# A hybrid decoder layer on one core: the gate's first weights, the routing's order and the final sums rearranged

## The chip, the cores and the metric

The kernel runs on one core of a Trainium2 chip, with its engines TensorE (PE), VectorE (DVE), ScalarE (ACT), GpSimd (POOL) and SyncE (SP), which here issues most loads. The metric is the device time of one execution in microseconds. Three executions of the kernel before took 1488.31, 1494.20 and 1494.39 us, median 1494.2.

## The reference

One decoder layer on 512 tokens of width 2048, in float32. A state-space group and a convolution group share one input projection; their outputs, side by side, go through one output projection. Then come a layer normalisation, a mixture of 32 experts, a second normalisation, a gated embedding and a third normalisation:

```python
h = layer_norm(DEEPNORM_ALPHA * x + y, ln1_g[i], ln1_b[i])
m = hierarchical_moe(h, w_rg[i], b_rg[i], w_re[i], b_re[i], w_gate[i], w_up[i], w_down[i])
h = layer_norm(DEEPNORM_ALPHA * h + m, ln2_g[i], ln2_b[i])
e = (p[i] @ w_p[i]) * jax.nn.sigmoid(h @ w_pg[i] + b_pg[i])
x = layer_norm(DEEPNORM_ALPHA * h + e, ln3_g[i], ln3_b[i])
```

In the mixture each token picks one of four groups by a softmax over 4 logits, two of that group's eight experts by a softmax over their logits, and adds the two experts' outputs with those weights. An expert is `silu(t @ w_gate) * (t @ w_up)` (width 256), times the weight, times `w_down`.

## The kernel before

Tokens lie in four tiles of 128 (`tt`, 2048 columns each). The program runs on five engines, each in its own order, with semaphores between them; the order on each engine is set by a scheduler that works through the code below with a timeline of its own, and by the pools of buffers, whose reuse makes waits.

Up to about 630 us: input projection, the two groups, output projection. Then the first normalisation of the four tiles, written to `h_dram`, and the routing on VectorE: the experts' one-hots (`oh`), counts and ranks by matmuls (`cc`, `cn`, `rk`), ranks of the experts by load (`gt`), each token's place (`hot`), and by matmul the slots' token rows (`sl0`) and weights (`wt0`). The embedding `p @ w_p` is computed in pieces (`embedding`, later L1177) and stored to `p_dram`. Its weights lie in the two raw places (`wps`).

The expert stage works in 14 groups of up to four experts with 128 slots in all. For a group GpSimd gathers 128 token rows from `h_dram` into `gx` (L1070), TensorE transposes them (L1084), multiplies with four quarters of `w_gu` (L1104, `up`), VectorE and ScalarE form the activations (`act`), TensorE multiplies with the two halves of `w_dn` (L1124, `down`), and GpSimd scatters each half of the result to `y_dram` (L1074), where every token has two rows. Each expert takes six loads of 1 MB, 192 in all. SyncE issues them in order (`ring_load`, L1066) into a ring of 17 places (15 of the stage's own and the two raw places, which join when the embedding's weights are done). Behind group 0, program text L1161 to L1181, stand the embedding of tiles 2 and 3 and the scaling of `tt` by ALPHA. Then comes a branch (L1189) for a case of overflow, which this data doesn't take; at it each engine waits for its own outstanding transfers.

The final stage loads each tile's two rows per token from `y_dram`, adds them to `tt`, takes statistics (L1334), normalises (L158 to L181), transposes (L1348), splits into a high and a low half (`h2h`, `h2l`, L79 and L80) and multiplies with the gate's weights `w_pg` (16 loads of 1 MB, split the same way into `whi` and `wlo`), three matmuls for each product (L100 to L102). The first four of these loads go to the two raw places and two places `fr`, with half of the splits on GpSimd. GpSimd also adds most of the rows (L1332, L1333).

Of the kernel before, what the change touches and what calls it, by code (L numbers as in the profile page):

```python
# [54 lines left out]
def build(tc, I, out, dbg=None, stages=9):  # L55
# [159 lines left out]
    sl0 = cpool.tile([P, 2 * NGR], I32, name="sl0")  # L215
    wt0 = cpool.tile([P, NGR], FT, name="wt0")
# [421 lines left out]
    if True:  # L638

        yhl = []  # L640

        def y_rows(n):

            y2 = s1.enter_context(tc.tile_pool(reuse_waits="tile", name=f"y2{n}", bufs=1))
            yhl.append([[y2.tile([P, 8, 2 * P], FR, name=f"y{n}{a}{g}") for a in "hl"] for g in range(2)])
# [139 lines left out]
        with ExitStack() as s3:  # L785
            w_o = ahead([lambda c=c, q=q: wsplit(wB if q % 2 else wA, raw_load(I["w_o"][c, q]), 4) for c in range(4) for q in range(2, 4)], 3)
            op_ = s3.enter_context(tc.tile_pool(reuse_waits="tile", name="op", bufs=1, side="right"))
            st1 = [op_.tile([P, 4, 6], FT, name=f"st{m}") for m in range(NT)]
# [39 lines left out]
            def embedding(m, x):  # L828

                z = op_.tile([P, 1], FT, name="pz0", bufs=1)  # L830
                V.tensor_scalar(z, x, 0.0, 0.0, op0=OP.is_equal, op1=OP.mult)
                pm = wB.tile([P, 2, P], FT, name="pm", tag="whi", bufs=4)
                A.activation(pm, pT[:, :, m * P:(m + 1) * P], AF.Identity, bias=z)
                for q in range(2):
                    pe_ = wB.tile([P, 2, 512], FT, name="pe", tag="wlo", bufs=4)
                    for c in range(2):
                        ps = bank("ops")
                        for k in range(2):
                            T.matmul(ps, pm[:, k], wps[q][:, k, c * 512:(c + 1) * 512], start=k == 0, stop=k == 1)
                        A.copy(pe_[:, c], ps)  # L840
                    G.dma_start(p_dram[m, 2 * q:2 * q + 2].rearrange("c p d -> p c d"), pe_)
# [19 lines left out]
            def finish(m):  # L861
                mean, rstd = ln_stats(op_, st1[m], "s")
                nm = op_.tile([P, 1], FT, name="nm", bufs=1)
                V.scalar_tensor_tensor(nm, mean, -1.0, rstd, op0=OP.mult, op1=OP.mult)
                lt = op_.tile([P, 36], FT, name="lt", bufs=2)
                V.scalar_tensor_tensor(lt, s12[:, 0:36], nm, s12[:, 36:72], op0=OP.mult, op1=OP.add)
                V.scalar_tensor_tensor(lg[:, m], lacc[m], rstd, lt, op0=OP.mult, op1=OP.add)
                if m < NT - 2:
                    normalize(m, mean, rstd)
                return m, mean, rstd  # L870

            def normalize(m, mean, rstd):
                for q in range(4):
                    i = slice(q * 512, (q + 1) * 512)
                    t = tt[m][:, i]
                    layer_norm(t, t, mean, rstd, g1[:, i], b1[:, i])
                G.dma_start(h_dram[m * P:(m + 1) * P], tt[m])
                dump("h", tt[m], lambda d: d[m * P:(m + 1) * P])
# [29 lines left out]
            pT = wB.tile([P, 2, S], FT, name="pT", tag="whi", bufs=4)  # L908
# [12 lines left out]
            rank = place[:, 0]  # L921
            gl = lg[:, :, 0:4]
            el = lg[:, :, 4:36]
            gmax, gsum, gprob, gmin = rt("gmax", NT), rt("gsum", NT), rt("gprob", NT), rt("gmin", NT)
            V.tensor_reduce(gmax, gl, axis=AX.X, op=OP.max)
            gmb = gmax.unsqueeze(2).broadcast_to([P, NT, 4])
            gd, ge, gs_, pen = rt("gd", NT, 4), rt("ge", NT, 4), rt("gs", NT, 4), rt("pen", NT, 4)
            V.tensor_tensor(gd, gl, gmb, op=OP.subtract)
            exp_of(rp, ge, gd, [P, NT, 4], "eg")
            V.tensor_reduce(gsum, ge, axis=AX.X, op=OP.add)  # L930
            V.reciprocal(gprob, gsum)

# [44 lines left out]
            V.tensor_scalar(gt, krow, kcol, None, op0=OP.is_lt)  # L977
            rr, rc = bank("ops"), bank("ops")
# [14 lines left out]
            embedding(0, rtok[:, 0:1])  # L993
# [44 lines left out]
            A.dma_start(sv_dram, sv.rearrange("p a n -> p (a n)"))  # L1038
            embedding(1, wt0[:, 0:1])
# [8 lines left out]
    if True:  # L1048
        psE = s5.enter_context(tc.tile_pool(reuse_waits="tile", name="psE", bufs=1, space=PSUM))
# [5 lines left out]
        def big(name):  # L1055
            return ep.tile([P, D], FT, name=name)

        ring = [big(f"ring{n}") for n in range(2, NRING)]
        xt = ep.tile([P, KD, P], FT, name="xt")
        gx, ob = big("gx"), big("ob")  # L1060
        turn = [0]
# [44 lines left out]
        def act(gu, w):  # L1106
            act = ep.tile([P, FH], FT, name="act")
            at = ep.tile([P, 2, P], FT, name="at", bufs=2)
# [40 lines left out]
        pm = ep.tile([P, 2, 2 * P], FT, name="pm")  # L1149
        nc.sync.dma_start(pm, I["pT"][:, :, 2 * P:])  # L1150
        gather(sl0[:, 0:1])
        V.tensor_copy(ids_, tab[:, 0:NP])
        columns()
        for i, (width, members) in enumerate(GROUPS):
# [11 lines left out]
            if i:  # L1166
                continue

            ahead1 = [loads(1, 0)]

            for m in range(2):
                for q in range(2):
                    pe_ = ep.tile([P, 2, 512], FT, name="pe")
                    for c in range(2):
                        ps = bank("dps", 4)
                        for k in range(2):
                            T.matmul(ps, pm[:, k, m * P:(m + 1) * P], wps[q][:, k, c * 512:(c + 1) * 512], start=k == 0, stop=k == 1)  # L1177
                        (A.copy if c else V.tensor_copy)(pe_[:, c], ps)
                    G.dma_start(p_dram[2 + m, 2 * q:2 * q + 2].rearrange("c p d -> p c d"), pe_)
            for m in range(NT):  # L1180
                A.mul(tt[m], tt[m], ALPHA)  # L1181
            ring.extend(rpool.tile([P, D], FT, name="raw", tag="raw", bufs=2) for _ in range(2))
            ahead1.append(loads(1, 1))

# [59 lines left out]

    s5.close()


    with ExitStack() as s5:
# [22 lines left out]

        raws = [rpool.tile([P, D], FT, name="raw", tag="raw", bufs=2) for _ in range(2)] + [fy.tile([P, D], FT, name=f"fr{n}") for n in range(2)]
        for q in range(3):
            nc.sync.dma_start(raws[q], I["w_pg"][0, q])
        y0 = [fy.tile([P, 2, 1024], FT, name=f"y0{c}") for c in range(2)]
        hls = [wsplit(wF, raws[q], 8, (V, V) if q else (G, G)) for q in range(3)]
# [41 lines left out]
        def total(m):  # L1318

            t = h2[m]  # L1320
            st2 = fh.tile([P, 4, 6], FT, name="st2", bufs=2)
            if m:
                rs = [rpool.tile([P, 2, 1024], FT, name="raw", tag="raw", bufs=2) for _ in range(2)]
                for c in range(2):
                    load_y(rs[c], m, c)
            else:
                rs = y0
            for c, r in enumerate(rs):
                for q in range(2):
                    i = slice(q * 512, (q + 1) * 512)  # L1330
                    o = t[:, c * 1024 + q * 512:c * 1024 + (q + 1) * 512]
# [23 lines left out]
        fystk.close()  # L1355
        fp = s5.enter_context(tc.tile_pool(reuse_waits="tile", name="fp", bufs=1))
# [109 lines left out]
```

## Time and profile before

| | |
|---|---|
| median of three executions | 1494.2 us |
| the profiled execution's own time | 1491.18 us |
| its span in the profile | 1489.4 us |
| busy: PE, DVE, POOL, ACT | 1264.2, 784.9, 394.9, 373.5 us |
| mean granted clock of TensorE | 0.932 of full speed |
| read from memory, written | 324.49 MB, 36.38 MB |

The profile is of one execution; durations below are of that one. A row with x4 merges four instructions, and its time runs from the first one's start to the last one's end. The bracket at a row's end is the idle time of the engine ahead of it and what ended that. SPq and the like are an engine's own queue work, such as issuing a DMA.

### The profile page before, as it was taken

The numbers are of one execution on the slowest core, as the hardware profiler recorded it, in microseconds if no ns is written. First come the engines' busy times: TensorE is split into PE (matmuls) and PEld (weight loads), VectorE is DVE, ScalarE is ACT, GpSimd is POOL, SyncE is SP. The second block draws the span as 40 slices with busy tenths as digits, with TensorE's granted clock in tenths as the row PEclk, the third lists the DMA queues.
The fourth block names the chain that finished last, engine by engine and source line by source line (L and its number), as shares of the span: only waits on it lengthen the run. The fifth ranks groups of instructions, "written<-read, shape, count | busy, mean of one in ns | idle before, by whom it ended". The sixth has DMA issues, their size and how long they took to land.

```text
span 1489.4 us, 16537 instructions
## 1 busy us (share of the span) xinstructions
PE 1264.2 (85%) x6128; PEld 809.5 (54%) x6129; DVE 784.9 (53%) x1258; ACT 373.5 (25%) x562; POOL 394.9 (27%) x330
## 2 busy tenths in 40 slices
PE   6999999999999999966758989987767675599996
PEld 4877877777777888843213333332111122388884
DVE  7999899789997643680101111110000006975567
ACT  4336555554333421121001111110000003023210
POOL 0368677864944200001101111100000005600000
PEclk9999999998999999958969999999998996699998
DMA  6344444436531351536779999999999985426413
GB/s 233 110 131 119 152 145 136 144 113 217 219 122 57 114 209 57 227 141 260 300 273 420 417 400 421 421 421 418 419 411 415 417 359 203 141 99 219 140 44 120
DMA packets 97176, 349.47 MB, mean 235 GB/s; under 512 B 30136, under 2 KB 43960, under 8 KB 61504
## 3 DMA queue, kind: packets, MB, share of 16 engines
q1 hardware_dynamic: 51152, 303.34, 52.6%
q10 hardware_dynamic: 38160, 19.82, 5.1%
q0 software_dynamic: 7776, 25.18, 4.3%
q8 instruction: 50, 0.82, 0.2%
q14 instruction: 38, 0.31, 0.1%
HBM read 324.49 MB, written 36.38 MB: 242 GB/s over the span
## 4 chain that ended last, share of the span: by engine, by line
PE 24%; DMA 19%; DVE 5%; issue 1%; ACT 1%; POOL 0%; DVEq 0%; SPq 0%; POOLq 0%
DMA ring<-w_gu 12%; PE gu L1104 7%; DMA ring<-w_dn 6%; PE dps L1124 4%; PE fps L102 3%; PE fps L100 3%; PE fps L101 3%; PE xtp L1084 1%; DMA gx<-h_dram,sl 1%; DVE tt L180 1%; DVE tt L181 1%; PE h2p L102 0%; PE h2p L100 0%; PE h2p L101 0%; DVE lnq L166 0%
## 5 line engine op out<-in xcount | busy, mean ns | idle before, releaser
L1104 PE MATMUL gu<-ring,xt 128*32 128x512 f32 (+2 forms) x1032 | 231.3, 634 | 42.6 <-DMA ring<-w_gu 42.6
L236 DVE SCALAR_TENSOR_TENSOR cps<-hc,wdw,cps 128x512 f32<-128x512 f32 x232 | 174.4, 752 | 4.8
L100 PE MATMUL zp<-xh,whi 128*128 128x512 f32 x384 | 157.7, 412 | 10.2 <-ACT whi L79 10.2
L79 ACT CAST whi<-raw 128x1024 fp32r<-128x1024 f32 x116 | 119.4, 1047 | 170.3 <-PE zp L102 51.3
L1104 PEld LDWEIGHTS gu<-ring,xt 128*32 128x32 f32 (+2 forms) x1032 | 62.6, 129 | 176.7 <-issue 101.5
L80 DVE TENSOR_TENSOR wlo<-raw,whi 128x1024 fp32r<-128x1024 f32 x90 | 126.6, 1416 | 57.4 <-ACT whi L79 56.4
L102 PE MATMUL zp<-xh,wlo 128*128 128x512 f32 x384 | 154.2, 402 | 3.0 <-DVE wlo L80 3.0
L101 PE MATMUL zp<-xl,whi 128*128 128x512 f32 x384 | 154.7, 403 | 1.6 <-DVE xl L80 1.6
L1124 PE MATMUL dps<-ring,at 128*32 128x512 f32 (+2 forms) x584 | 132.3, 619 | 13.0 <-DMA ring<-w_dn 6.5
L1110 DVE TENSOR_TENSOR act<-act,gu 128x256 f32<-128x256 f32 x14 | 5.9, 422 | 217.0 <-ACT act L1109 217.0
L1074 POOL DMA_INDIRECT y_dram<-ob,sl x28 | 27.9, 995 | 321.7 <-ACT ob L1126 321.7
L1089 DVE COPY xt<-xtp 128x512 f32<-128x512 f32 x28 | 19.4, 692 | 155.6 <-PE xtp L1084 146.9
L80 POOL TENSOR_TENSOR wlo<-raw,whi 128x1024 fp32r<-128x1024 f32 x26 | 69.5, 2675 | 87.2 <-ACT whi L79 74.7
L100 PE MATMUL fps<-whi,h2h 128*128 128x512 f32 x224 | 89.8, 402 | 1.0 <-ACT h2h L79 1.0
L102 PE MATMUL fps<-whi,h2l 128*128 128x512 f32 x224 | 89.8, 402 | 0.0
L101 PE MATMUL fps<-wlo,h2h 128*128 128x512 f32 x224 | 89.1, 399 | 0.0
L1124 PEld LDWEIGHTS dps<-ring,at 128*32 128x32 f32 (+2 forms) x584 | 38.2, 128 | 91.6 <-issue 63.2
L100 PEld LDWEIGHTS zp<-xh,whi 128*128 128x128 f32 x384 | 73.5, 192 | 25.9 <-ACT whi L79 10.3
L102 PEld LDWEIGHTS zp<-xh,wlo 128*128 128x128 f32 x384 | 73.3, 191 | 21.1 <-DVE wlo L80 4.2
L101 PEld LDWEIGHTS zp<-xl,whi 128*128 128x128 f32 x384 | 73.6, 192 | 17.2 <-DVE xl L80 2.0
L1126 DVE COPY ob<-dps 128x512 f32<-128x512 f32 x28 | 19.4, 692 | 111.9 <-PE dps L1124 106.4
L1084 PE MATMUL xtp<-ident,gx 128*128 128x128 f32 x224 | 38.2, 296 | 44.3 <-DMA gx<-h_dram,sl 32.5
(451 smaller groups left out, 2283.6 us busy)
## 6 DMA issues: line engine op xcount, KB each, us to landing
ring<-w_gu SPq DMA_DIRECT2D x109, 1024.0 KB, 20.7
ring<-w_dn SPq DMA_DIRECT2D x61, 1024.0 KB, 19.8
raw<-w_in SPq DMA_DIRECT2D x24, 1024.0 KB, 5.0
raw<-w_gu SPq DMA_DIRECT2D x19, 1024.0 KB, 20.1
raw<-w_o SPq DMA_DIRECT2D x16, 1024.0 KB, 5.0
raw<-w_pg SPq DMA_DIRECT2D x14, 1024.0 KB, 5.1
raw<-y_dram SPq DMA_DIRECT2D x12, 512.0 KB, 5.6
raw<-xT SPq DMA_DIRECT2D x4, 1024.0 KB, 5.1
```

The costliest lines, as they stand in the source:

```text
L79: A.copy(hi, src)
L80: eng.tensor_tensor(lo, src, hi.bitcast(FT), op=OP.subtract)
L100: T.matmul(ps, lh, rh, start=start, stop=False)
L101: T.matmul(ps, lh, rl, start=False, stop=False)
L102: T.matmul(ps, ll, rh, start=False, stop=stop)
L236: V.scalar_tensor_tensor(ps if k < 30 else acc, hc[:, k:k + S], wdw[:, ct, k:k + 1], ps, op0=OP.mult, op1=OP.add)
L1074: G.indirect_dma_start(out=y_dram[q], out_offset=bass.IndirectOffsetOnAxis(ap=isc, axis=0), in_=ob[:, q * 1024:(q + 1) * 1024], in_offset= ...
L1084: T.transpose(ps[:, kk * P:(kk + 1) * P], gx[:, k * P:(k + 1) * P], ident)
L1089: V.tensor_copy(o, ps)
L1104: T.matmul(gu[cols], xt[:, k, cols], raws[j][:, kk * 512:(kk + 1) * 512], start=k == 0, stop=k == KD - 1)
L1124: T.matmul(outs[c][cols], at[:, k, cols], raws[j][:, o:o + 512], start=k == 0, stop=k == 1)
L1126: (A.copy if c else V.tensor_copy)(ob[:, q * 1024 + c * 512:q * 1024 + (c + 1) * 512], outs[c])
```

## The change

1. Of the first normalisation, tiles 2 and 3 are taken out of the stretch ahead of the routing and given to VectorE in pieces between the routing's steps, each held back by a value of the step it follows. The exponentials of the weights follow the slots' rows. The first gather takes its rows from a copy of its own, `sl1`, and the clearing of `gx` goes.
2. The embedding is cut into pieces of half a tile. Six of eight stand ahead of the experts, the last three of them stored from ScalarE's queue; tile 3's two stand behind group 1's `down`, on the raw places' weights. Scaling by ALPHA moves to group 2.
3. The ring has another order: 15 places in `ep` and two `kept` places in a pool that lives on into the final stage. The raw places join at its head behind tile 3's embedding. The last 17 loads pass over the kept and raw places, which take the gate's first four loads.
4. In the final stage, tile 0's first rows and all rows of the other tiles are added into `tt` by GpSimd's accumulating DMAs, tile 0's second rows by a plain load and VectorE. Tiles 1 to 3 wait at a one-column instruction for tile 0. The splits on GpSimd go to ScalarE and VectorE.

The diff, cut to its core:

```diff
+            embedding(0, 0, lacc[NT - 1][:, 0:1])
...
-            for d in done[NT - 2:]:
-                normalize(*d)
+            for q in range(2):
+                normalize(2, q, *done[2], oh[:, 0, 0:1])
...
+            for q in range(4):
+                normalize(3, q, *done[3], hot[:, 0, 0:1])
...
+            V.tensor_scalar(sl1, sz[:, 0:1], float(S - 1), None, op0=OP.min)
+            for n, (m, q) in enumerate(((1, 1), (2, 0), (2, 1))):
+                embedding(m, q, sz[:, n:n + 1], A)
...
+        kept = [kp.tile([P, D], FT, name=f"kept{n}") for n in range(2)]
+        ring = [ring[0], *ring[4:], *kept, last, ring[1], ring[2], ring[3]]
...
         def ring_load(src):
-            t = ring[turn[0] % NRING]
-            turn[0] += 1
+            count[0] += 1
+            t = ring.pop(0)
+
+            while count[0] > 6 * NE - NRING and any(t is k for k in kept):
+                t = ring.pop(0)
+            ring.append(t)
             nc.sync.dma_start(t, src)
...
-            for m in range(2):
+            if i == 1:
+
                 for q in range(2):
...
+                kept += [rpool.tile([P, D], FT, name="raw", tag="raw", bufs=2) for _ in range(2)]
+                ring[:0] = kept[2:]
...
+        for q in range(4):
+            V.tensor_copy(kept[q][:, 0:1], at_[(NGR + 1) % 2][:, 0, 0:1])
+            nc.sync.dma_start(kept[q], I["w_pg"][0, q])
...
+        def add_y(m, j):
+
+            for c in range(2):
+                G.dma_start(h2[m][:, c * 1024:(c + 1) * 1024], yv[c][m, :, j], accum_op=OP.add)
...
+        add_y(0, 0)
+        for m in range(1, NT):
+
+            o = h2[m].rearrange("p (c d) -> p c d", c=2)[:, :, 0]
+            V.scalar_tensor_tensor(o, h2[0][:, 0:2], 0.0, o, op0=OP.mult, op1=OP.add)
+        for m, j in ((1, 0), (2, 0), (1, 1), (3, 0), (2, 1), (3, 1)):
+            add_y(m, j)
+        hls += [wsplit(wF, kept[q], 8) for q in range(2, 4)]
...
-                    (G if m or q == 0 else V).tensor_tensor(r[:, 0, i], r[:, 0, i], r[:, 1, i], op=OP.add)
-                    (G if m and not (m == 1 and q) else V).tensor_tensor(o, o, r[:, 0, i], op=OP.add)
-                    V.bn_stats(st2[:, 2 * c + q], o)
+            for q in range(4):
+                o = t[:, q * 512:(q + 1) * 512]
+                if m == 0:
+                    V.tensor_tensor(o, o, y1[:, q * 512:(q + 1) * 512], op=OP.add)
+                V.bn_stats(st2[:, q], o)
```

Three places of the instruction order, each before and after. On SyncE at the branch (L1189), before; a load's target is a place of the ring or a raw place, with a buffer's number behind it, and register instructions between the loads are left out.

```order
L1066 DMA ring8_5521<-w_dn 128x2048
L1066 DMA raw_5695<-w_gu 128x2048
L1066 DMA raw_5696<-w_gu 128x2048
L1189 UNCONDITIONAL_BRANCH
L1066 DMA ring9_5522<-w_gu 128x2048
L1066 DMA ring10_5523<-w_gu 128x2048
L1066 DMA ring11_5524<-w_gu 128x2048
L1066 DMA ring12_5525<-w_gu 128x2048
L1066 DMA ring13_5526<-w_dn 128x2048
```

And now (the branch is L1233):

```order
L1112 DMA ring10_5573<-w_dn 128x2048
L1112 DMA ring11_5574<-w_dn 128x2048
L1233 UNCONDITIONAL_BRANCH
L1112 DMA raw_6359<-w_gu 128x2048
L1112 DMA raw_6360<-w_gu 128x2048
L1112 DMA kept0_5585<-w_gu 128x2048
L1112 DMA kept1_5586<-w_gu 128x2048
L1112 DMA ring12_5583<-w_dn 128x2048
L1112 DMA ring1_5564<-w_dn 128x2048
L1112 DMA ring2_5565<-w_gu 128x2048
```

The raw loads have moved from ahead of the branch to behind it, where they precede all other loads. Each waits for the last matmul of tile 3's embedding (L1216) that reads its place.

On SyncE at the end of the expert stage, before: the last expert loads, then the gate's.

```order
L1066 DMA ring2_5515<-w_gu 128x2048
L1066 DMA ring3_5516<-w_dn 128x2048
L1066 DMA ring4_5517<-w_dn 128x2048
L1066 DMA ring5_5518<-w_dn 128x2048
L1066 DMA ring6_5519<-w_dn 128x2048
L1274 DMA raw_8223<-w_pg 128x2048
L1274 DMA raw_8224<-w_pg 128x2048
L1267 DMA fsg0_8209<-ln2 8x512
L1274 DMA fr0_8225<-w_pg 128x2048
```

And now, from the fifth w_gu load of the last group on:

```order
L1112 DMA ring6_5569<-w_gu 128x2048
L1292 DMA kept0_5585<-w_pg 128x2048
L1292 DMA kept1_5586<-w_pg 128x2048
L1292 DMA raw_6359<-w_pg 128x2048
L1292 DMA raw_6360<-w_pg 128x2048
L1112 DMA ring7_5570<-w_gu 128x2048
L1112 DMA ring8_5571<-w_gu 128x2048
L1112 DMA ring9_5572<-w_gu 128x2048
L1112 DMA ring10_5573<-w_dn 128x2048
L1112 DMA ring11_5574<-w_dn 128x2048
L1112 DMA ring12_5583<-w_dn 128x2048
```

The gate's four loads (w_pg) have moved ahead of the last seven expert loads.

On VectorE at tile 0's last statistics and the start of its reciprocal square root, before (tt_3353 is tile 0):

```order
L1334 BN_STATS st_8293<-tt_3353 128x6 x2
L1333 TENSOR_TENSOR tt_3353<-tt_3353,y_8231 128x512
L1334 BN_STATS st_8293<-tt_3353 128x6
L176 BN_AGGR lnmv<-st_8293 128x2
L158 TENSOR_SCALAR lnu<-lnmv 128x1
L180 SCALAR_TENSOR_TENSOR tt_3353<-tt_3353,lnmv,g_8205 128x512
L159 CAST lnf<-lnu 128x1
L160 TENSOR_SCALAR lnf<-lnf 128x1
```

And now (tt_3354 is tile 0, tt_3355 is tile 1):

```order
L1378 BN_STATS st_8308<-tt_3354 128x6 x2
L176 BN_AGGR lnmv<-st_8308 128x2
L158 TENSOR_SCALAR lnu<-lnmv 128x1
L180 SCALAR_TENSOR_TENSOR tt_3354<-tt_3354,lnmv,g_8214 128x512
L159 CAST lnf<-lnu 128x1
L1378 BN_STATS st_8431<-tt_3355 128x6 x2
L160 TENSOR_SCALAR lnf<-lnf 128x1
L163 TENSOR_SCALAR lnu<-lnu 128x1
```

Two statistics of tile 1 have moved into the middle of tile 0's steps.

## Rows read from the trace of the kernel before

**Rows 1.** Stretches: span, length, busy PE, PEld, DVE, ACT, POOL, PEclk, DMA share, GB/s

```profile
800.00:1215.00 415.00, 332.68 (x1751) 105.03 (x1751) 40.38 (x66) 34.51 (x67) 33.22 (x33) 0.96 1.01 416
1215.00:1242.00 27.00, 23.17 (x84) 8.07 (x81) 3.04 (x6) 4.58 (x7) 3.34 (x3) 0.88 0.59 221
1242.00:1304.00 62.00, 29.35 (x88) 18.18 (x88) 59.87 (x73) 12.51 (x20) 42.36 (x28) 0.61 0.48 169
1304.00:1476.00 172.00, 170.32 (x757) 140.18 (x755) 111.54 (x194) 40.34 (x50) 0.00 (x0) 0.98 0.37 127
```

**Rows 2.** SyncE's waits over the span: us in total, times, longest

```profile
SPq L1066 <- DMA ring<-w_gu: 135.8, 61, 3.5
```

**Rows 3.** Order in time, SyncE, 1183 to 1256: start us, us, line, operation

```profile
1184.19 10.27 SPq L1066 DMA_DIRECT2D ring<-w_gu  x5
...
1196.73 2.70 SPq L1066 DMA_DIRECT2D raw<-w_gu  x2
...
1205.27 8.57 SPq L1066 DMA_DIRECT2D ring<-w_dn  x4
...
1222.49 4.47 SPq L1274 DMA_DIRECT2D raw<-w_pg  x2
```

**Rows 4.** Chain that ended last, 1190 to 1490: start us, us, what

```profile
1236.18 5.44 DMA y_dram<-ob,sl
...
1474.60 0.70 DVE fsg L1306
```

**Rows 5.** Order in time, TensorE, 1266 to 1325

```profile
1269.40 1.11 PE L1348 MATMUL h2p<-ident,tt 128*128 128x128 f32 x4 [18.14 <-DVE tt L181]
```

**Rows 6.** Order in time, GpSimd and TensorE, 715 to 765

```profile
724.53 0.99 POOL L1074 DMA_INDIRECT y_dram<-ob,sl  x1 [2.39 <-ACT ob L1126]
...
749.71 1.08 POOL L1070 DMA_INDIRECT gx<-h_dram,sl  x1 [0.31 <-issue]
...
762.46 1.09 PE L1084 MATMUL xtp<-ident,gx 128*128 128x128 f32 x4 [22.48 <-DMA gx<-h_dram,sl]
```

**Rows 7.** DMA issues by line: count, us to landing

```profile
y_dram<-ob,sl POOLq DMA_INDIRECT x28, 8.3
```

**Rows 8.** Chain, 640 to 830

```profile
793.15 1.00 PE dps L1124 x2
```

**Rows 9.** Order in time, SyncE, 595 to 792

```profile
600.58 64.22 SPq L1066 DMA_DIRECT2D ring<-w_gu  x8
...
712.95 2.21 SPq L1066 DMA_DIRECT2D ring<-w_dn  x4
...
734.15 6.19 SPq L1066 DMA_DIRECT2D raw<-w_gu  x2
...
748.40 2.27 SPq L1066 DMA_DIRECT2D ring<-w_gu  x4
...
750.87 20.82 SPq L1066 DMA_DIRECT2D ring<-w_dn  x2
...
780.27 9.22 SPq L1066 DMA_DIRECT2D ring<-w_gu  x4
```

**Rows 10.** Line L1066, 770 to 800

```profile
DMA to landing us min/median/max: 4.9/11.6/16.6
```

**Rows 11.** Order in time, TensorE, 1176 to 1200

```profile
1187.61 3.39 PE L1124 MATMUL dps<-ring,at 128*32 128x512 f32 x12 [0.46 <-ACT at L1115]
```

**Rows 12.** Order in time, VectorE, 1236 to 1310

```profile
1248.54 2.35 DVE L80 TENSOR_TENSOR wlo<-fr,whi 128x1024 fp32r<-128x1024 f32 x2
...
1269.45 2.08 DVE L180 SCALAR_TENSOR_TENSOR tt<-tt,mean,g 128x512 f32<-128x512 f32 x3
...
1292.26 4.88 DVE L180 SCALAR_TENSOR_TENSOR tt<-tt,mean,g 128x512 f32<-128x512 f32 x3
...
1302.69 1.27 DVE L80 TENSOR_TENSOR h2l<-h2p,h2h 128x512 fp32r<-128x512 f32 x2
```

**Rows 13.** Line L841, GpSimd's stores of the embedding

```profile
DMA to landing us min/median/max: 3.1/4.9/6.2
```

More of the change, by code (lines that the diff above doesn't have):

```diff
@@ L215, in build @@
     sl0 = cpool.tile([P, 2 * NGR], I32, name="sl0")
+    sl1 = cpool.tile([P, 1], I32, name="sl1")
     wt0 = cpool.tile([P, NGR], FT, name="wt0")
@@ L825, in build, with zero_of, embedding @@
             V.tensor_reduce(kbc, kd_, axis=AX.X, op=OP.add)
-            def embedding(m, x):
-                z = op_.tile([P, 1], FT, name="pz0", bufs=1)
+            def zero_of(x):
+                z = zp.tile([P, 1], FT, name="pz0", bufs=2)
                 V.tensor_scalar(z, x, 0.0, 0.0, op0=OP.is_equal, op1=OP.mult)
[L832 to L841, printed above, removed]
+                return z
+            def embedding(m, q, x, eng=G):
+                eturn[0] ^= 1
+                pm = pms[eturn[0]]
+                A.activation(pm, pT[:, :, m * P:(m + 1) * P], AF.Identity, bias=zero_of(x))
+                pe_ = pes[eturn[0]]
+                for c in range(2):
+                    ps = bank("ops")
+                    for k in range(2):
+                        T.matmul(ps, pm[:, k], wps[q][:, k, c * 512:(c + 1) * 512], start=k == 0, stop=k == 1)
+                    A.copy(pe_[:, c], ps)
+                eng.dma_start(p_dram[m, 2 * q:2 * q + 2].rearrange("c p d -> p c d"), pe_)
             def logits(m, c):
@@ L868, in finish, with normalize @@
                 if m < NT - 2:
[L869 to L878, printed above, removed]
+                    for q in range(4):
+                        normalize(m, q, mean, rstd)
+                return mean, rstd
+            def normalize(m, q, mean, rstd, x=None):
+                if x is not None:
+                    late = op_.tile([P, 1], FT, name="late", bufs=1)
+                    V.scalar_tensor_tensor(late, x, 0.0, mean, op0=OP.mult, op1=OP.add)
+                    mean = late
+                i = slice(q * 512, (q + 1) * 512)
+                t = tt[m][:, i]
+                layer_norm(t, t, mean, rstd, g1[:, i], b1[:, i])
+                if q == 3:
+                    G.dma_start(h_dram[m * P:(m + 1) * P], tt[m])
+                    dump("h", tt[m], lambda d: d[m * P:(m + 1) * P])
             for c in range(4):
@@ L907, in build @@
                         done.append(finish(m))
-            pT = wB.tile([P, 2, S], FT, name="pT", tag="whi", bufs=4)
+            eturn = [0]
+            eh, el_ = (ypools[0].tile([P, D], FT, name=f"e{a}", tag=f"y0{a}1") for a in "hl")
+            pT = el_[:, 0:1024].rearrange("p (k t) -> p k t", k=2)
+            pms = [el_[:, 1024 + 256 * n:1280 + 256 * n].rearrange("p (k t) -> p k t", k=2) for n in range(2)]
+            pes = [eh[:, 1024 * n:1024 * n + 1024].rearrange("p (c d) -> p c d", c=2) for n in range(2)]
             nc.sync.dma_start(pT, I["pT"])
@@ L977, in build @@
             V.tensor_scalar(gt, krow, kcol, None, op0=OP.is_lt)
+            for q in range(2, 4):
+                normalize(2, q, *done[2], cn[:, 0:1])
             rr, rc = bank("ops"), bank("ops")
@@ L1048, in build @@
     if True:
+        kstk = top.enter_context(ExitStack())
+        kp = kstk.enter_context(tc.tile_pool(reuse_waits="tile", name="kp", bufs=1, side="right"))
         psE = s5.enter_context(tc.tile_pool(reuse_waits="tile", name="psE", bufs=1, space=PSUM))
@@ L1056, in big @@
             return ep.tile([P, D], FT, name=name)
-        ring = [big(f"ring{n}") for n in range(2, NRING)]
+        ring = [big(f"ring{n}") for n in range(12)]
         xt = ep.tile([P, KD, P], FT, name="xt")
-        gx, ob = big("gx"), big("ob")
-        turn = [0]
-        def ring_load(src):
-            t = ring[turn[0] % NRING]
-            turn[0] += 1
+        ob = big("ob")
+        at_ = [ep.tile([P, 2, P], FT, name=f"at{n}") for n in range(2)]
+        act_ = ep.tile([P, FH], FT, name="act")
+        pm = ep.tile([P, 2, P], FT, name="pm")
+        pe_ = ep.tile([P, 2, 512], FT, name="pe")
+        ids_ = ep.tile([P, NP], I32, name="ids")
+        last = big("ring12")
+        gx = big("gx")
+        kept = [kp.tile([P, D], FT, name=f"kept{n}") for n in range(2)]
+        ring = [ring[0], *ring[4:], *kept, last, ring[1], ring[2], ring[3]]
+        turn, count = [0], [0]
+        def ring_load(src):
+            count[0] += 1
[3 more added lines that the diff above has]
+            ring.append(t)
             nc.sync.dma_start(t, src)
@@ L1106, in act @@
         def act(gu, w):
[L1107 to L1108 removed]
+            act = act_
+            turn[0] ^= 1
+            at = at_[turn[0]]
             A.activation(act, gu[:, 0:FH], AF.Sigmoid)
@@ L1148, in build @@
         early = [loads(0, q) for q in range(6)]
-        pm = ep.tile([P, 2, 2 * P], FT, name="pm")
-        nc.sync.dma_start(pm, I["pT"][:, :, 2 * P:])
-        gather(sl0[:, 0:1])
+        ahead1 = [loads(1, 0)]
+        gather(sl1)
         V.tensor_copy(ids_, tab[:, 0:NP])
@@ L1176, in build @@
                         for k in range(2):
-                            T.matmul(ps, pm[:, k, m * P:(m + 1) * P], wps[q][:, k, c * 512:(c + 1) * 512], start=k == 0, stop=k == 1)
+                            T.matmul(ps, pm[:, k], wps[q][:, k, c * 512:(c + 1) * 512], start=k == 0, stop=k == 1)
                         (A.copy if c else V.tensor_copy)(pe_[:, c], ps)
[L1179 to L1182, printed above, removed]
+                    G.dma_start(p_dram[NT - 1, 2 * q:2 * q + 2].rearrange("c p d -> p c d"), pe_)
+                kept += [rpool.tile([P, D], FT, name="raw", tag="raw", bufs=2) for _ in range(2)]
+                ring[:0] = kept[2:]
+            if i == 2:
+                for m in range(NT):
+                    A.activation(tt[m], tt[m], AF.Identity, scale=ALPHA, bias=zero_of(at[:, 0, 0:1]))
+            if i:
+                continue
             ahead1.append(loads(1, 1))
+            nc.sync.dma_start(pm, I["pT"][:, :, (NT - 1) * P:])
             mo = xt[:, 0, 0:1].bitcast(I32)
@@ L1270, in build @@
             V.tensor_copy(pick[n], ident[0:8, 4 * n:4 * n + 4].unsqueeze(2).broadcast_to([8, 4, P]))
[L1272 to L1276, printed above, removed]
+        y1 = fy.tile([P, D], FT, name="y1")
+        hls = [wsplit(wF, kept[q], 8) for q in range(2)]
         for n in range(8):
```

61 lines of the change are left out of this document (24 added, 37 removed).

## The prediction

> **What bounds the kernel now.** I read stretches cut at the stage borders first, then SyncE's waits, since it issues the weight loads, then those loads in time, then the chain of what ended last, and at last TensorE and VectorE behind the experts.
>
> From 800 to 1215 us DMA is busy at a share of 1.01 and moves 416 GB/s, while PE works 332.7 of 415 us [rows 1]: the stream of expert weights, 192 loads of 1 MB, bounds the expert stage. SyncE's longest waits of its own in that stage are for a load's landing, 61 times for a w_gu load [rows 2]: a load is issued when an earlier one is down. Late in the stage five are issued in 10.27 us, a gap of (10.27 - 0.33)/4 = 2.49 us each [rows 3]. One load more or less in a full stream moves the experts' end by that. The chain ends this stage with the last scatter's 5.44 us, down at 1241.6 [rows 4]; I call that moment E.
>
> Behind E another engine binds. From 1242 to 1304 VectorE is busy 59.9 of 62 us and PE 29.4; from 1304 to 1476 PE is busy 170.3 of 172 us [rows 1]. PE's first transposes of the final stage come at 1269.40, after 18.1 us of waiting for VectorE's normalisation [rows 5].
>
> **The change part by part.**
>
> *Routing and the first two groups.* Normalisation of two tiles leaves the way of the routing chain, and the clearing of gx before the first gather goes, while three more pieces of the embedding stand ahead of group 0's transposes on TensorE. Adding these up I estimate that group 0 starts about 7 us earlier. Of the four embedding pieces behind it (L1177) two go ahead of it and two behind group 1; with them goes the train of stores on GpSimd that lets the second gather start at 749.71 only [rows 6]. That gather can now go when group 0's scatters are down. The later one was issued at 724.53 [rows 6], now near 717.5, and lands 8.3 us after that at the median [rows 7]: near 726, so the gather starts some 23 us earlier, near 727. Its landing took from 749.71 to 762.4 [rows 6], beside five loads; without them I take 8, so TensorE starts group 1 near 735. Group 1 took from 762.46 to 794.15 [rows 6, 8], 31.7 us, and now ends near 768.
>
> *What the load queue makes of it.* This is the step that I weigh most. Before issues 24 loads by 740.3, after the branch five more into free places from 748.40 to 751.2, and the next at 771.4, as TensorE frees places: 29 loads are out before 771 [rows 9]. In the new order the first two loads after the branch go into the two raw places. These hold the embedding's weights until tile 3's embedding has run on TensorE, and that one now stands behind group 1's down projection. SyncE issues in order, so the kept places, ring12 and ring1 to ring3, all free, stand behind that wait. Only 24 loads (15 early, 9 refills) are out before it, and the 25th goes near 769.5. From there 4.9 us to land, the least in this stretch [rows 10], and 13 more gaps of 2.49 make 806.8 for load 38; tile 3's embedding stores 1 MB in the same time, 2.5 us more: 809.3. Before, load 38 was the last of the four issued from 780.27 to 789.49 [rows 9], at 789.16, and with 11.6 us to landing [rows 10] it is down at 800.8. The third gather and nearly all of group 1's scatters are done by then in both kernels. So the stream is 8.5 us late. Bounds: nothing, if the lead isn't needed, and 5 loads x 2.49 = 12.4 us. I take 8.5, since DMA is full from there to 1215. The 23 us that TensorE wins are lost: it will wait for loads.
>
> *The gate's first weights.* Before, its loads are issued behind all expert loads, from 1222.49 on [rows 3], when the stream is running out (DMA share 0.59 from 1215 to 1242 [rows 1]). In the new order all four stand ahead of the last seven expert loads on SyncE's queue. They wait only for group 12's activations; its down projection starts at 1187.61 [rows 11], before the sixth load of group 13, which they now precede, was issued at 1196.73 [rows 3]. So they don't stall, they take 4 x 2.49 = 10.0 us of a full stream, and the last w_dn load lands that much later. Bounds: 0 if there is slack, and 4 x 2.75 = 11.0 by the spacing of the last w_dn issues, (8.57 - 0.33)/3 [rows 3]. I take 10.0. They give nothing back behind E, where the wait that ended last at 1269.40 was for VectorE's normalisation, not for these weights [rows 5]. That the last loads have thirteen places instead of seventeen I cost at nothing: an earlier load's landing, not a free place, is what SyncE waits for most [rows 2]; if that cover goes, each place missed is again 2.49 us.
>
> *Behind E.* GpSimd's adds and splits go (42.4 us busy of 62 [rows 1]), and the sums of the rows come by 14 accumulating DMAs of 0.52 MB. VectorE takes all eight low halves of the first weights, two in 2.35 us. What VectorE gains: three steps of L180 took 2.08 us with GpSimd waiting and 4.88 us beside its adds [rows 12]. I add its new order up. An accumulate is down 3.1 to 4.9 us after its issue if it goes as GpSimd's plain stores do [rows 13], so tile 0's are down and its gate instruction through near E+6. Then, up to the first low half of tile 1: 7 splits x 1.2 = 8.4, 22 scale steps x 0.69 = 15.2, 24 adds, statistics and low halves of 512 columns x 0.64 = 15.4, and some 40 one-column steps, 5.5 by estimate; sum 44.5, so E+50.5. Before, that half came at 1302.69 = E+61.1 [rows 12]. From there TensorE has work without a stop in both. This is 9 to 10 us gained, if tile 1's rows are there when VectorE asks for them: their statistics now stand ahead of tile 0's rsqrt, near E+20.5, and need the ninth accumulate. At the rate of the full stream (0.52 MB at 416 GB/s, 1.25 us) that lands near E+18. No row prices an accumulate. At 2.5 us each the ninth lands near E+28.5 and the gain shrinks to 1.5; one after the other at 4.9 us [rows 13], near E+50, a loss of 20. The nearest rows are plain transfers, which overlap: I take a rate between the first two, and a gain of 6.
>
> The Trainium skill ("Collectives: The Full Stack", section "The bandwidth ceiling: the fold count and why AG ≠ RS ≠ AR") says that an add in the DMA reads two sources for each write, and so runs at about half a copy's rate there. By that rule the gain of this part is 1.5 instead of 6; no row here shows it, and it speaks against the change.
>
> *Sum.* E comes 8.5 + 10.0 later, the stage behind it is 6 shorter: 12.5 on the profiled execution's own 1491.2 us (span 1489.4 and 1.8 around it), 1503.7. The 14.8 us from the last gate step at 1474.60 to the end [rows 4] stay. That execution lies 3.0 below the median of 1494.2 (runs from 1488.3 to 1494.4). My added-up start of group 1 is more likely late than early, so I round down to 1502.
>
> **Rivals.**
>
> *One: TensorE, not the loads, bounds the experts (the faster side).* For it: the chain of group 1 runs on TensorE up to 794.15, where a piece of group 1 ends without a wait for a load [rows 8]. Against it: PE is busy 80% from 800 to 1215 beside a DMA share of 1.01 [rows 1]. Then neither the held-up queue nor the gate's four loads count, and -9 behind E is left: 1482. It decides from the point at which the last group's loads land before TensorE asks for them.
>
> *Two: the hold-up of the queue is made good, the gate's loads are not.* If group 1 ends some 8 us before 768, load 38 is on time: +10 - 9 = +1, 1492. For it: my 768 rests on an added-up 727. Against it: the raw places stand behind group 1 whenever it starts.
>
> *Three: accumulates at 2.5 us or more.* VectorE stands ahead of tile 0's rsqrt and waits for tile 1's rows: 18.5 - 1.5 = 17, 1508; at 3.8 us each the ninth lands near E+38 and it is 18.5 + 8, 1518. For it: the trace before shows no accumulate at all. Against it: plain transfers overlap.
>
> **How the numbers follow.** A measurement of this kernel can tell about 0.5% from no change, 7.5 us: 1486.7 to 1501.7. Forecast 0.44, its own range 1496 to 1508, two thirds of it above 1501.7. Rival one 0.17 (1480 to 1490, mostly faster), rival two 0.22 (same), rival three 0.17 (slower). Slower: 0.29 + 0.17 = 0.46; faster 0.14; same the rest, 0.40. The range that leaves out two in ten is 1486 to 1513.
>
> **What the new profile would show.** Right: SyncE waiting on TensorE for a raw place to near 770, DMA idle from about 737 to 770; four w_pg loads issued between 1195 and 1215, and the last scatter down near 1260; no adds on GpSimd, L180 at 0.7 us throughout, and a shorter gap of PE ahead of tile 1. Wrong: the last scatter at 1250 or before (the loads were not the limit, or the gate's loads rode in slack), or VectorE idle ahead of tile 0's rsqrt behind a DMA (slow accumulates).

## The result, and the profile after

The changed kernel takes 1499.44 us (median of 7 runs, 1497.36 to 1501.89); the kernel before, measured beside it, 1488.31 (median of 7 with the three shown above, 1486.86 to 1494.39). The ratio is 1.0072, 95% interval 1.0055 to 1.0089: slower by 11 us. The prediction said 1502, range 1486 to 1513, slower at 0.46.

The profiled execution has a span of 1499.8 us against 1489.4, 10.4 more. Stretches of the changed kernel (the columns of [rows 1]):

```profile
733.00:771.00 38.00, 32.13 (x133) 12.56 (x130) 4.87 (x8) 4.17 (x8) 4.86 (x5) 0.99 0.40 136
...
600.00:800.00 200.00, 158.69 (x656) 81.01 (x658) 69.05 (x245) 32.30 (x50) 18.11 (x21) 0.87 0.67 261
```

and of its later part, with borders moved with the stages:

```profile
800.00:1215.00 415.00, 320.05 (x1657) 96.94 (x1648) 36.85 (x64) 30.71 (x60) 29.08 (x29) 0.95 1.01 417
1215.00:1242.00 27.00, 15.02 (x48) 4.30 (x45) 0.90 (x2) 0.76 (x2) 0.00 (x0) 0.69 0.61 241
...
1320.00:1486.00 166.00, 164.89 (x743) 135.85 (x741) 98.58 (x152) 39.23 (x49) 0.00 (x0) 1.00 0.35 124
```

From 800 to 1215 the stream is full, as before. From 733 to 771 DMA is used to 0.40 only. Yet over 600 to 800 it is 0.67 at 261 GB/s, and in the kernel before:

```profile
600.00:800.00 200.00, 142.20 (x577) 77.54 (x576) 66.18 (x225) 26.94 (x39) 17.39 (x20) 0.81 0.67 261
```

The same: the kernel before idles earlier, with a share of 0.52 against 0.64 from 600 to 692 and 0.68 against 0.40 from 733 to 771. TensorE's first transposes of group 0, before and after, and the matmuls of tile 3's embedding behind group 1, after:

```profile
692.74 1.08 PE L1084 MATMUL xtp<-ident,gx 128*128 128x128 f32 x4 [10.01 <-DMA gx<-h_dram,sl]
```

```profile
672.10 0.66 PE L1130 MATMUL xtp<-ident,gx 128*128 128x128 f32 x4
...
757.55 7.13 PE L1216 MATMUL dps<-raw,pm 128*128 128x512 f32 x16
```

SyncE at the branch and at the end of the expert stage, after (start, length, line, operation, count; compare [rows 9] and [rows 3]):

```profile
761.29 3.77 SPq L1112 DMA_DIRECT2D raw<-w_gu  x2
765.29 1.26 SPq L1112 DMA_DIRECT2D kept<-w_gu  x2
```

```profile
1183.91 10.25 SPq L1112 DMA_DIRECT2D ring<-w_gu  x5
1196.27 2.81 SPq L1292 DMA_DIRECT2D kept<-w_pg  x2
1201.71 3.54 SPq L1292 DMA_DIRECT2D raw<-w_pg  x2
1207.47 6.06 SPq L1112 DMA_DIRECT2D ring<-w_gu  x3
1216.14 7.76 SPq L1112 DMA_DIRECT2D ring<-w_dn  x4
```

The raw loads go at 761.29 and the free places behind them from 765.29 on. SyncE waited for the raw places on TensorE, 38.4 us in two waits, the longer of 35.6:

```profile
SPq L1112 <- PE dps L1216: 38.4, 2, 35.6
```

The last group's first loads go at 1183.91, before at 1184.19 [rows 3]: up to here the stream is on time. The gate's four loads go from 1196.27 to 1205.25, between the fifth and the sixth load of that group. GpSimd around E, after:

```profile
1250.66 0.97 POOL L1120 DMA_INDIRECT y_dram<-ob,sl  x1 [2.49 <-ACT ob L1173]
1251.63 1.02 POOL L1331 DMA_DIRECT2D tt<-y_dram  x1
1253.62 0.87 POOL L1331 DMA_DIRECT2D tt<-y_dram  x1 [0.98 <-DMA y_dram<-ob,sl]
1258.18 5.19 POOL L1331 DMA_DIRECT2D tt<-y_dram  x6 [3.69 <-DVE tt L1339]
```

The accumulate at 1253.62 was released by the last scatter, so E is near 1253.3; it was 1241.6 [rows 4]. E is 11.7 later, and from E to the end of the span it is 246.5 instead of 247.8: 1.3 less. TensorE and VectorE behind E, after ([rows 5], [rows 12]):

```profile
1228.45 10.02 PE L1150 MATMUL gu<-ring,xt 128*64 128x512 f32 x30 [9.98 <-DMA ring<-w_gu]
...
1240.88 8.83 PE L1171 MATMUL dps<-ring,at 128*64 128x512 f32 x32 [0.46 <-ACT at L1162]
```

```profile
1289.33 1.09 PE L1392 MATMUL h2p<-ident,tt 128*128 128x128 f32 x4 [27.08 <-issue]
```

```profile
1271.83 0.15 DVE L159 CAST lnf<-lnu 128x1 f32<-128x1 int32 x1
1285.50 1.29 DVE L1378 BATCH_NORM_STATS2 st<-tt 128x6 f32<-128x512 f32 x2 [13.53 <-DMA tt<-y_dram]
...
1289.33 2.08 DVE L180 SCALAR_TENSOR_TENSOR tt<-tt,mean,g 128x512 f32<-128x512 f32 x3
...
1306.64 2.07 DVE L180 SCALAR_TENSOR_TENSOR tt<-tt,mean,g 128x512 f32<-128x512 f32 x3
...
1313.44 0.68 DVE L80 TENSOR_TENSOR h2l<-h2p,h2h 128x512 fp32r<-128x512 f32 x1
```

VectorE stands 13.53 us at tile 1's statistics, ahead of tile 0's rsqrt, for an accumulate. Three L180 now take some 2.07 us each time, and tile 1's first low half comes at 1313.44, E+60.1; it was E+61.1.

### The profile page after: what moved, and what is told of

Its sections match the earlier page's. It is cut to its first block, busy times and chain, and to the rows that moved or that the text cites. A ratio compares the mean times of both kernels' runs of the same rounds, so it can differ in the third digit from the quotient of the medians.

```text
span 1499.8 us, 16496 instructions
## 1 busy us (share of the span) xinstructions
PE 1269.5 (85%) x6128; PEld 807.2 (54%) x6129; DVE 758.1 (51%) x1282; ACT 376.7 (25%) x568; POOL 360.0 (24%) x313
## 4 chain that ended last, share of the span: by engine, by line
DMA 33%; PE 15%; DVE 3%; issue 0%; ACT 0%; SPq 0%; DVEq 0%; ACTq 0%; POOL 0%; POOLq 0%
DMA ring<-w_gu 18%; DMA ring<-w_dn 7%; PE fps L102 3%; PE fps L100 3%; PE fps L101 3%; DMA kept<-w_gu 2%; DMA tt<-y_dram 2%; PE gu L1150 2%; DMA raw<-w_dn 2%; DMA raw<-w_gu 2%; PE dps L1171 1%; DMA gx<-h_dram,sl 1%; DVE tt L180 1%; DVE st L1378 0%; DVE tt L181 0%; PE h2p L102 0%
## 5 line engine op out<-in xcount | busy, mean ns | idle before, releaser
L1150 PE MATMUL gu<-ring,xt 128*32 128x512 f32 (+2 forms) x984 | 218.0, 651 | 58.0 <-DMA ring<-w_gu 57.9
L1150 PEld LDWEIGHTS gu<-ring,xt 128*32 128x32 f32 (+2 forms) x984 | 54.6, 129 | 190.5 <-DMA ring<-w_gu 95.2
L80 DVE TENSOR_TENSOR wlo<-raw,whi 128x1024 fp32r<-128x1024 f32 x92 | 121.4, 1330 | 52.0 <-ACT whi L79 51.1
L1171 PE MATMUL dps<-ring,at 128*32 128x512 f32 (+2 forms) x488 | 115.9, 616 | 11.8 <-DMA ring<-w_dn 6.3
L80 POOL TENSOR_TENSOR wlo<-raw,whi 128x1024 fp32r<-128x1024 f32 x24 | 66.3, 2761 | 84.9 <-ACT whi L79 72.4
L101 PEld LDWEIGHTS zp<-xl,whi 128*128 128x128 f32 x384 | 74.1, 193 | 17.4 <-DVE xl L80 2.0
L1171 PEld LDWEIGHTS dps<-ring,at 128*32 128x32 f32 (+2 forms) x488 | 34.3, 126 | 76.6 <-issue 50.4
```

The source lines that it names most:

```text
L80: eng.tensor_tensor(lo, src, hi.bitcast(FT), op=OP.subtract)
L101: T.matmul(ps, lh, rl, start=False, stop=False)
L1150: T.matmul(gu[cols], xt[:, k, cols], raws[j][:, kk * 512:(kk + 1) * 512], start=k == 0, stop=k == KD - 1)
L1171: T.matmul(outs[c][cols], at[:, k, cols], raws[j][:, o:o + 512], start=k == 0, stop=k == 1)
```

## The experiments

All are edits of the changed kernel, timed in five rounds beside the kernel before.

| run | median us | ratio to before, 95% interval | last scatter down (E), profiled | from E to the end of the span |
|---|---|---|---|---|
| kernel before | 1488.3 | | 1241.6 | 247.8 |
| changed kernel | 1499.4 | 1.0072 (1.0055 to 1.0089) | 1253.3 | 246.5 |
| gate's loads last | 1493.3 | 1.0010 (0.9988 to 1.0032) | 1246.6 | 248.9 |
| gate's loads left out | 1488.1 | 0.9990 (0.9970 to 1.0009) | 1242.7 | 246.9 |
| two ahead, two behind | 1493.9 | 1.0040 (1.0023 to 1.0058) | 1246.8 | 247.4 |
| raw places last | 1475.7 | 0.9882 (0.9852 to 0.9913) | 1227.8 | 246.6 |
| first gather held back | 1512.2 | 1.0131 (1.0097 to 1.0165) | 1268.0 | 246.0 |
| plain transfers for accumulates | 1491.1 | 0.9992 (0.9971 to 1.0013) | 1251.1 | 237.0 |
| statistics held back | 1482.0 | 0.9934 (0.9913 to 0.9956) | 1253.9 | 227.5 |
| raw last, gate last, held back | 1446.1 | 0.9721 (0.9699 to 0.9743) | 1214.4 | 229.1 |
| raw last, gate mixed, held back | 1448.5 | 0.9730 (0.9709 to 0.9752) | 1219.0 | 227.7 |

The kernel before had medians of 1488.31 to 1490.44 in these groups of runs, so a difference of 2 us between groups is noise. The differences below are of medians. The ratios compare each run with the kernel before beside it, and by them, each to some 4 us, the gate's loads last are 9 us shorter than the changed kernel, left out 12 and mixed 5, the raw places last 28, plain transfers 12 and the statistics held back 21 shorter, and the gather held back is 9 longer. A profile is of one execution, and the stretch ahead of all edits varies too: GpSimd's store to `sv_dram`, shortly ahead of the first gather, goes at 662.76 in the changed kernel's profile, the earliest of all, and up to 7.6 us later in those of the edits.

### The gate's first loads

```diff
-            V.tensor_copy(kept[q][:, 0:1], at_[(NGR + 1) % 2][:, 0, 0:1])
+            V.tensor_copy(kept[q][:, 0:1], at_[NGR % 2][:, 0, 0:1])
```

> The changed kernel, but the gate's four first loads wait for the last group's activations instead of group 12's, so they stand behind all expert loads. Theory (they take 10.0 us of a full stream, and TensorE, idle meanwhile at the lower clock, does the last group slower): the last w_dn load lands near 1233.5 instead of 1243.2 and the last scatter near 1242 instead of 1253.3; the whole is 10 to 11 us shorter, near 1488. Rival (the loads rode in slack, the end moved for another reason): no change, 1499.

Measured: 6 us shorter (9 by the ratios), where 10 to 11 were expected. The last scatter is down at 1246.6. SyncE and GpSimd, this run:

```profile
1207.60 8.56 SPq L1112 DMA_DIRECT2D ring<-w_dn  x4
1232.28 0.82 SPq L1292 DMA_DIRECT2D kept<-w_pg  x2
1233.19 1.05 SPq L1292 DMA_DIRECT2D raw<-w_pg  x2
```

```profile
1238.43 0.97 POOL L1120 DMA_INDIRECT y_dram<-ob,sl  x1 [28.59 <-ACT ob L1173]
...
1246.05 1.89 POOL L1331 DMA_DIRECT2D tt<-y_dram  x2 [3.19 <-DMA y_dram<-ob,sl]
```

The w_dn loads go 8.5 us earlier than with the four ahead of them. But the gate's loads now go at 1232, 6 us ahead of the first scatter at 1238.43, whose landing GpSimd still waits for at 1246.05. They have moved from the stream into the tail, which is 248.9 us long instead of 246.5. To price them alone, the next run has them left out:

```diff
-            nc.sync.dma_start(kept[q], I["w_pg"][0, q])
```

> The changed kernel without the gate's first four loads (the gate multiplies by what the kept and raw places hold, so that part of the output is left out); their splits and all else stay. Theory (they take 10 us of a full stream and cost TensorE 2 us more): the last w_dn load lands near 1233.5, the last scatter near 1242, the whole near 1488, 11 to 12 us shorter, and more than with the loads put last, which then share the memory with the scatter and the first accumulates. Rival (they rode in slack): 1499.

Measured: 1488.1, 11.3 shorter, the last scatter at 1242.7 (10.6 earlier): as expected. At a ratio of 0.9990 the kernel is back at the time of the one before, so these four loads make up all that the change loses, and its other parts together neither win nor lose. TensorE's last group shows where the time beyond 10 comes from, without the loads and (shown above at 1228.45) with them:

```profile
1219.11 3.65 PE L1150 MATMUL gu<-ring,xt 128*64 128x512 f32 x16 [1.40 <-DMA ring<-w_gu]
1224.13 3.65 PE L1150 MATMUL gu<-ring,xt 128*64 128x512 f32 x14 [1.37 <-DMA ring<-w_gu]
...
1230.19 8.83 PE L1171 MATMUL dps<-ring,at 128*64 128x512 f32 x32 [0.46 <-ACT at L1162]
```

```profile
1215.00:1242.00 27.00, 22.03 (x83) 7.54 (x80) 4.17 (x7) 4.24 (x7) 2.96 (x3) 0.94 0.30 114
```

Without them, the last quarters of the up projection take 3.65 us for 14 to 16 matmuls, 0.23 to 0.26 each, with waits of 1.4 for a load. With them, TensorE idles 9.98 and then does 30 in 10.02, 0.33 each. The granted clock from 1215 to 1242 is 0.94 of full speed without and 0.69 with: of its two levels, 2.4 and 1.2 GHz, the lower had a larger share, after ten idle microseconds of TensorE. How large it is differs from execution to execution: in the two runs on the accumulates and on VectorE's order below, which have the loads ahead as well, the same 30 matmuls took 8.78 and 9.54 us after 11.37 idle. A dose between:

```diff
+            if i == NGR - 2:
+                for q in range(4):
+                    V.tensor_copy(kept[q][:, 0:1], ob[:, 1024:1025])
...
-            V.tensor_copy(kept[q][:, 0:1], at_[(NGR + 1) % 2][:, 0, 0:1])
             nc.sync.dma_start(kept[q], I["w_pg"][0, q])
```

> The changed kernel with the gate's first loads waiting for group 12's second result half: two of the four now stand ahead of the last three w_dn loads, two behind all. Theory (each load ahead of the last expert load costs 2.49 us): the last w_dn lands 5 us earlier than with four ahead, near 1238.3, and the last scatter 5 to 7 us earlier. Rival (what costs is the break in TensorE's work, not the place in the queue): less than 2 us.

Measured: 5.5 shorter, the last scatter 6.5 earlier, as expected. The two that went behind the expert loads give back about half.

### The loads behind the branch

```diff
-                ring[:0] = kept[2:]
+                ring += kept[2:]
```

> The changed kernel, but the two raw places join the ring behind the free places, not ahead of them. Theory as predicted (the queue's hold-up costs 8.5 us of a stream that is full afterwards): six loads go near 736 instead of after 765, DMA is busy in the stretch in which it idled, the last scatter lands 8 us earlier or more, 1491 or less. Rival (the hold-up costs nothing, since the gathers and scatters of groups 1 to 3 were done in that idle stretch and the stream is on time at the end): 1499, within 2 us.

Measured: 24 us shorter, 1475.7, three times what I had for it. Stretches of this run, and the store to `sv_dram`:

```profile
600.00:800.00 200.00, 161.41 (x676) 85.04 (x676) 71.03 (x249) 32.74 (x51) 17.03 (x20) 0.90 0.78 311
733.00:771.00 38.00, 36.06 (x138) 13.18 (x137) 4.36 (x7) 4.27 (x8) 3.81 (x4) 0.94 0.99 399
...
607.61:807.61 200.00, 161.41 (x707) 81.14 (x710) 68.76 (x245) 32.25 (x50) 18.08 (x21) 0.90 0.82 326
```

```profile
670.37 0.55 POOL L1069 DMA_DIRECT2D sv_dram<-scr  x1 [1.66 <-DVE scr L1052]
```

DMA is used to 0.99 from 733 to 771 instead of 0.40, and the last scatter is down 25.5 earlier. This execution was 7.6 us behind the changed kernel's ahead of the edit already (670.37 against 662.76). So the same stretch of the program is 607.6 to 807.6, where the share is 0.82 instead of 0.67: 0.15 x 200 = 30 us of idle DMA filled, and from that common point the last scatter is down 33.1 earlier. SyncE now waits for places as TensorE frees them. So the hold-up costs its whole idle stretch. What I had wrong was the comparison with the kernel before, which has an idle stretch of the same sum. Whether the loss depends on when group 1 ends, the next run asks:

```diff
+        for _ in range(4):
+            G.tensor_copy(gx, sl1.bitcast(FT).broadcast_to([P, D]))
         gather(sl1)
```

> The changed kernel with four copies into gx on GpSimd ahead of the first gather, which holds back groups 0 and 1 by their time, some 8 to 14 us. Theory (the loads stand behind group 1's end, so each microsecond by which group 1 ends later is a microsecond more of idle DMA, and that the changed kernel was no worse here than the one before is due to its earlier group 1): the first raw load goes that much later than 761.3 and the last scatter moves by the same 8 to 14 us, whole time 1507 or more. Rival (the stream makes the hold-up good by the end, whatever its length): the last scatter stays within 3 us, whole time 1499 to 1502.

Measured: 1512.2, 12.8 longer (9 by the ratios). The store to `sv_dram` and the first gather in the changed kernel's profile, and then GpSimd and stretches of this run:

```profile
662.76 0.55 POOL L1069 DMA_DIRECT2D sv_dram<-scr  x1 [1.66 <-DVE scr L1052]
665.59 1.09 POOL L1116 DMA_INDIRECT gx<-h_dram,sl  x1 [2.28 <-PE xp L846]
```

```profile
669.25 0.55 POOL L1069 DMA_DIRECT2D sv_dram<-scr  x1 [1.67 <-DVE scr L1052]
669.80 7.76 POOL L1196 COPY gx<-sl 128x2048 f32<-128x2048 f32 x4
677.85 1.10 POOL L1116 DMA_INDIRECT gx<-h_dram,sl  x1 [0.29 <-POOL gx L1196]
```

```profile
733.00:771.00 38.00, 29.86 (x129) 11.35 (x130) 4.87 (x8) 3.00 (x6) 2.03 (x2) 0.82 0.22 87
...
600.00:800.00 200.00, 152.38 (x620) 81.17 (x619) 68.81 (x241) 23.36 (x43) 22.54 (x22) 0.86 0.60 230
...
606.49:806.49 200.00, 150.91 (x603) 78.05 (x602) 67.91 (x243) 26.39 (x46) 23.62 (x23) 0.86 0.63 244
```

The gather goes 12.3 later and the last scatter is down 14.7 later, but this execution was 6.5 us behind ahead of the copies already (669.25 against 662.76). The copies themselves hold the gather back by 5.8 us, the first raw load (775.64 against 761.29) by 7.9 and the last scatter by 8.2. Over the same stretch of the program, 606.5 to 806.5, DMA is used to 0.63 instead of 0.67: 0.04 x 200 = 8 us less. The stream makes nothing good.

### The accumulates and VectorE's order

```diff
-                G.dma_start(h2[m][:, c * 1024:(c + 1) * 1024], yv[c][m, :, j], accum_op=OP.add)
+                G.dma_start(h2[m][:, c * 1024:(c + 1) * 1024], yv[c][m, :, j])
```

> The changed kernel with the 14 accumulating transfers as plain ones: the sums of the experts' rows with the residual are left out, all transfers, waits and instructions stay. Theory (an accumulate of 0.52 MB takes about 2.5 us where a plain one takes 1.25): they land 1.3 us apart instead of 2.45, VectorE's wait of 13.5 us ahead of tile 0's rsqrt shrinks to under 4, and the whole is 8 to 10 us shorter, near 1490. Rival (the spacing is GpSimd's issuing, 0.85 us and more each, or its waits for earlier landings): spacing and time stay, 1499.

Measured: 1491.1, 8.3 shorter. Line L1331 of the changed kernel, and then of this run:

```profile
L1331 POOL DMA_DIRECT2D tt<-y_dram x14: 839/862/2496, 1251.6 to 1283.2; - x14
...
DMA to landing us min/median/max: 6.1/15.3/22.1
```

```profile
L1331 POOL DMA_DIRECT2D tt<-y_dram x14: 528/528/599, 1249.6 to 1271.2; - x14
...
DMA to landing us min/median/max: 4.1/10.2/14.1
```

```profile
1274.07 1.29 DVE L1378 BATCH_NORM_STATS2 st<-tt 128x6 f32<-128x512 f32 x2 [6.08 <-DMA tt<-y_dram]
```

VectorE's wait is 6.08 instead of 13.53, where under 4 was expected. The last six land 1.28 us apart when plain (1274.0 to 1280.4) and 2.45 us apart when they accumulate (1285.5 to 1297.8). From E to the end it is 237.0 us, 9.5 shorter. That E comes 2.2 earlier too lies ahead of any accumulate: in this execution the last group's up and down matmuls took 8.78 and 7.40 us, against 10.02 and 8.83.

```diff
+            if m:
+                x = h2l[:, KD - 1, P - 1:P].bitcast(FT) if m == 1 else h2[m - 1][:, D - 1:D]
+                V.tensor_scalar(st2[:, :, 0], x.broadcast_to([P, 4]), 0.0, None, op0=OP.mult)
             for q in range(4):
```

> The changed kernel with each later tile's statistics held back on VectorE until the tile before is normalised; the accumulates stay. Theory (the loss behind the experts is only that tile 0's chain stands behind tile 1's rows): tile 0's transposes come near 1275 instead of 1289, tile 1's first low half near 1297 instead of 1313, the whole is 12 to 16 us shorter, near 1485. Rival (the accumulates themselves are too late for TensorE, whatever the order): tile 1's low half stays beyond 1308 and the gain is under 5 us.

Measured: 1482.0, 17.4 shorter, a little beyond the range, with the accumulates as slow as ever. This run's TensorE and VectorE:

```profile
1275.11 1.09 PE L1395 MATMUL h2p<-ident,tt 128*128 128x128 f32 x4 [12.41 <-issue]
```

```profile
1287.75 1.29 DVE L1381 BATCH_NORM_STATS2 st<-tt 128x6 f32<-128x512 f32 x2 [0.42 <-DMA tt<-y_dram]
...
1295.52 0.68 DVE L80 TENSOR_TENSOR h2l<-h2p,h2h 128x512 fp32r<-128x512 f32 x1
```

Tile 0 goes to TensorE at 1275.11 instead of 1289.33, and when VectorE comes to tile 1's rows it waits 0.42 us for them; tile 1's first low half comes at 1295.52 instead of 1313.44, E+41.6 instead of E+60.1.

### All together

> Raw places last, gate's loads behind all expert loads, later tiles' statistics held back, all three. If the three losses lie in three stages and add, -24 - 6 - 18 from 1499: near 1452. If the gate's loads and the accumulates get into each other's way behind the experts, as the single edit suggests, no better than 1458.

> Raw places last, two of the gate's loads ahead of the last three w_dn loads and two behind, later tiles' statistics held back. By sums -24 - 5 - 18 from 1499: near 1452 to 1455, as the version with all four behind or a little better, since less is under way when the scatter and the accumulates go.

Measured: 1446.1 and 1448.5, 2.8% and 2.7% below the kernel before and better than the sums, which were of medians from other groups of runs; by the ratios the single edits sum to 58 and 54 us, and together they give 52 and 51. So they add within what the groups differ by, and the table shows why: they lie in three stages. E comes 38.9 and 34.3 earlier than in the changed kernel, and from E to the end it is 229.1 and 227.7, as with the statistics alone. A collision of the gate's loads with the accumulates isn't shown: the last scatter takes 6.2 us to land in the first and 2.7 in the changed kernel, but 5.7 in the second too, where the gate's loads were issued some 16 us ahead of the last group's first scatter. The two differ by no more than their runs do.

## Why the prediction was right or wrong

- *The direction and the time* were right, the time in part by luck: two of three terms of the sum were off, on opposite sides, and nearly cancel. It had E +18.5 and -6 behind it; measured +11.7 and -1.3. By the medians the difference is 11.1 us (1499.4 less 1488.3), where the sum has 12.5.
- *The gate's first weights: right.* I took 10.0 us; left out, they give 10.6 at E and 11.3 in all. What the term lacked is TensorE's lower clock after the idle stretch that they make. The fewer places for the last loads, taken at nothing, cost nothing that shows: with the four left out the kernel takes the time of the one before.
- *The load queue: the step that failed.* Its mechanism was right (SyncE held by the raw places behind group 1, DMA used to 0.40 meanwhile), and its size, 8.5 against the kernel before, should have been near 0: the last group's first loads go at 1183.91 against 1184.19, and at 1184.52 to 1186.51 in the five runs that differ from the changed kernel only behind that point. I counted loads from 733 on. Load 38 is as late as I said (load 39, issued at 786.83, lands 24.7 later at 811.5, so load 38 near 809), but by chance. Group 0 starts 20.6 us earlier on TensorE (672.10 against 692.74), not 7, group 1's down projection ends near 757.6, not 768, and the raw loads go 8.2 us earlier than I had added up (761.3, not 769.5). From there to load 38 it takes some 48 us, not 39.8, and the two errors of 8 us cancel. By then two more gathers and a pair of scatters are done than before, since they moved into the idle stretch. Over 600 to 800 both kernels use DMA to 0.67. A sum over that whole stretch, not a race to one load, would have told it.
- *Rival one* (TensorE bounds the experts) is refuted by two runs: the last scatter moves with the idle DMA, 33.1 earlier for 30 us filled and 8.2 later for 8 added, nearly one for one. *Rival two's* path came true: the hold-up is made good against before, the gate's loads are not. Its time, 1492, did not, for the gain behind E failed as rival three had it. The two together, +10 and -1.5 on 1491.2, make 1499.7.
- *Behind E: the size failed, on the side of rival three.* VectorE's own work is as short as I summed it or shorter: with the statistics held back, tile 1's first low half came at E+41.6, where I had E+50.5. The accumulates cost 2.45 us each, the far one of the two rates between which I took mine, at which I had a gain of 1.5; measured 1.3. The Trainium skill's rule ("Collectives: The Full Stack", section "The bandwidth ceiling: the fold count and why AG ≠ RS ≠ AR"), given there for collectives, that an add with two source reads runs at about half a copy's rate, agrees with this trace: 2.45 against 1.28 us. I gave it 0.17 and should have taken it.
- *Slips in the sums.* Group 1's 31.7 us from 735 on make 766.7, not 768; 61.1 less 50.5 is 10.6, not 9 to 10; at 3.8 us each the ninth accumulate lands near E+40, not E+38. None changes the outcome.
- Not tried: rows of the other tiles added in another order, and the routing's part by itself. That the earlier groups 0 and 1 are what pays for the hold-up rests on the equal shares over 600 to 800 and on the run with the gather held back.

## What to carry to other kernels

Where one stream of loads bounds a stage, count what its engines leave idle over the whole way up to the point where it is full; that sum, not the first late load, is what the end moves by. A load that must wait belongs behind those that need not, on a queue that issues in order, and a load that isn't needed yet behind the last one that is. When a slow transfer replaces work on an engine, look at what stands behind its first reader in that engine's order: holding that reader back cost one small instruction a tile and gave 17 us.

## What the runs showed of the hardware that I had not expected

An accumulating DMA of 0.52 MB from HBM into SBUF took 2.45 us in a run of them, a plain one of the same shape 1.28; to issue one took GpSimd 0.86 us at the median against 0.53 plain. And the gate's four loads were dearer than the 10.0 us of their transfer by 0.6 us at E and 1.3 in all; in the profiles TensorE's last 30 up matmuls then took 0.33 us each instead of 0.23 to 0.26, at a granted clock of 0.69 instead of 0.94.
